# Hybrid encoder, one core: opening sums on column tiles, three projection groups by quarters, GpSimd's tensor work on VectorE

## The chip, the cores and the metric

One core of one Trainium2 chip runs the whole kernel. The metric is device time in microseconds; the kernel before takes 831.13 us, the median of three runs (829.75 to 832.08). Matrices are float32; a product is made either directly in fp32, which TensorE does in two passes, or from a split of both operands into a high part (fp32r) and a low part, which takes three passes: high by high, high by low, low by high.

## The reference, cut to what matters

Two layers work on x of 256 tokens by 1024 channels. The conditioning vector c (1024) gives scale, shift and gate for both sub-layers by one matrix product.

```
mod = silu(c) @ ada_w + ada_b                      # ada_w (1024, 6144)
sh_m, sc_m, g_m, sh_f, sc_f, g_f = split(mod, 6)
h = rms_norm(x, norm_mix_g) * (1 + sc_m) + sh_m
proj = h @ w_in                                    # qa ka va | cq ckv kr | qc | kc vc | ga gb gc
o_na  = neighborhood_attention(qa, ka, va, rpb)    # 4 heads of 64
o_mla = attention from rms_norm(cq) @ w_uq, rms_norm(ckv) @ w_ukv, rope(kr)   # 4 heads
o_gqa = attention from rms_norm + axial rope of qc, kc; vc                    # 8 heads, 2 kv heads
merged = sig(ga)*(o_na @ w_na) + sig(gb)*(o_mla @ w_mla) + sig(gc)*(o_gqa @ w_gqa)
x = x + g_m * (merged @ w_out)
h = rms_norm(x, norm_ffn_g) * (1 + sc_f) + sh_f
x = x + g_f * ((silu(gate) * up) @ w_down)         # gate, up = split(h @ w_gate_up)
```

After two layers a last rms_norm gives the output.

## The kernel before, in words

**Items.** A projection is a *group* (line 285): up to 512 output columns, contracted in units of 256 rows. Each unit is an *item*: one weight tile of 128 x 2 x 512, loaded on SP's queue, split by `load_split` (line 269; high part on ScalarE, line 215, low part on VectorE, line 216), and used in two *steps*, one per 128 tokens (t = 0, 1). A step of a split item is 6 matmuls (lines 305 to 307); of an item marked native, 2 fp32 matmuls in two passes each (line 298). After the last unit the group's `post` function reads the accumulated bank.

**Order of the work.** The loop at the end walks the items: it runs the side work hung on that item (`at`), loads and splits, runs the first step and keeps the second back until four items are pending (LAG); for the first eight items the second step follows at once. `later(k, f)` puts f k steps back; `flush` empties the pending steps. This order is a priority: the framework that builds the program schedules each engine's instructions from it, so that a ready instruction may pass one that waits. SP's queue issues all loads.

**The opening of layer 0.** `first_a` loads the first quarter of the scale columns (two tiles of 512 KB), x, and the first quarter of the shift columns; it takes the sum of squares of x on ScalarE (line 220), scales x on VectorE (230), transposes it on TensorE (237) and copies it to SBUF (877). `first_q(q)` treats a quarter, 256 of the 1024 columns of scale and shift: `ada_quarter_dve` (148) multiplies weight tiles by the conditioning column and accumulates on VectorE (lines 137, 139), 8 operations of 128 x 256 per quarter of scale or shift, then reduces over partitions by transposes (121) and a VectorE reduction (123). Quarter 0 of shift alone goes through TensorE as a row (161, 167). Then ScalarE makes the modulated operand hF (894), and it is split for later groups. Groups g1 (columns 768 to 1183) and ga (0 to 511) are native and interleaved by quarters: items 0 to 7. Group gc (keys and values, split) follows as items 8 to 11, then w_uq, w_ukv, and gd (queries of the grouped attention) as items 14 to 17; six gate groups follow and, spread among them, the attention pairs in the order na, mla, gqa.

**GpSimd** does the rotary tables of `params` (363, 369; at item 0), the bias of the neighbourhood attention (386; at item 8, after four loads of 256 KB), the rotary key of the latent attention (428 to 432), the merge adds (706), the last norm's product (827), and small powers for the norms (107). The merge (line 695 on) multiplies each branch by its gate on VectorE (701, 705), adds on GpSimd (706), and transposes the sum on TensorE (715) for w_out.

**PSUM** has eight banks: four for groups (`psmm`), three for transposes and the like (`tpb`), one for attention outputs (`pso`).

The lines that the steps rest on:

```python
def group(...):                               # line 305 on, for each of 2 row blocks of a unit
    nc.tensor.matmul(ps[t], lhs(t, 0, kc), hi[:, j, 0:n], ...)
    nc.tensor.matmul(ps[t], lhs(t, 0, kc), lo[:, j, 0:n], ...)
    nc.tensor.matmul(ps[t], lhs(t, 1, kc), hi[:, j, 0:n], ...)
# attention output: two heads on two column tiles, line 666
nc.tensor.matmul(ov[i * 64:(i + 1) * 64, j, :], v, ptTs[i][:, k, :], ...)
```

Of the kernel before, what the change touches and what calls it, by code (L numbers as in the profile page):

```python
# [31 lines left out]
SD = 2  # L32
# [5 lines left out]
def encoder_kernel(ctx: ExitStack, tc: tile.TileContext, x, consts, cols, rows, ada_b, rpb, ada_w, w_in,  # L38
# [102 lines left out]

    def ada_quarter_load(l, m, q, u):
        c0 = m * D + q * 256
        raw = t4([P, 4, 256])
        nc.sync.dma_start(raw, ada_w[l, u * 512:(u + 1) * 512, c0:c0 + 256].rearrange("(k p) n -> p k n", p=P))
        return raw

    def ada_quarter_dve(l, ms, q, raws):
        accs = {m: modp.tile([P, 512], F32, tag="acc", name=nm("acc"))[:, 0:256] for m in ms}
        for kc in range(KC):  # L150
            for m in ms:
                ada_acc(accs[m], raws[(m, kc // 4)][:, kc % 4:kc % 4 + 1, :], kc, 1)
        for m in ms:
            col_mod(l, m, q * 2, 2, accs[m])

    def ada_quarter_pe(l, m, q, raws):
        if (l, m) not in mods:
            mods[(l, m)] = modp.tile([P, KC], F32, tag=f"c{m}", name=nm("cm"))
        ps = tpb()
        for kc in range(KC):  # L160
            nc.tensor.matmul(ps[0:1, 0:256], sc[:, kc:kc + 1], raws[(m, kc // 4)][:, kc % 4, :], start=(kc == 0),
                             stop=(kc == KC - 1))
        row = t2([1, 256])
        nc.scalar.copy(row, ps[0:1, 0:256])
        pc = tpb()
        for j in range(2):
            nc.tensor.matmul(pc[:, j:j + 1], row[0:1, j * P:(j + 1) * P], ones[0:1, 0:1], start=True, stop=True)
        nc.vector.tensor_tensor(out=mods[(l, m)][:, q * 2:q * 2 + 2], in0=pc[:, 0:2],
                                in1=colp(l, "b", m * KC + q * 2, 2), op=ALU.add)
# [115 lines left out]
    def group(units_src, nkc, n, lhs, post, kc0=0, pres=None):  # L285
# [3 lines left out]
        for u in range(nu):  # L289
            nk = min(2, nkc - 2 * u)  # L290

            def mm(t, it, u=u, nk=nk):
                if u == 0:
                    ps[t] = psmm.tile([P, 512], F32, tag="mm", name=nm("mm"))
                if it.get("native"):
                    for j in range(nk):
                        kc = 2 * u + j
                        nc.tensor.matmul(ps[t][:, 0:n], state["hF"][kc // 4][:, kc % 4, t * P:(t + 1) * P],  # L298
                                         it["w"][:, j, 0:n], start=(kc == 0), stop=(kc == nkc - 1))
                    return  # L300
# [45 lines left out]
    def layer(l):  # L346
# [6 lines left out]
        def params():  # L353
# [5 lines left out]
            for nme, g0 in (("q", 0), ("k", 64)):  # L359
# [3 lines left out]
                nc.gpsimd.tensor_tensor(out=gC, in0=axC, in1=g.unsqueeze(1).to_broadcast([P, NT, 64]), op=ALU.mult)  # L363
# [11 lines left out]
        def na_bias():  # L375
            st["bias"] = []
            for t in range(NT):
# [622 lines left out]
```

## Time and profile before

| | us |
|---|---|
| median of three runs | 831.13 |
| lowest, highest | 829.75, 832.08 |
| the profiled execution's own time | 831.54 |
| its span, first to last instruction | 829.7 |
| mean granted TensorE clock | 0.991 |

The profile is of one execution. In the rows below, PE is TensorE's matmul side, PEld its weight loads, DVE is VectorE, ACT ScalarE, POOL GpSimd; L12 is line 12. Times are us from the start of the span. A matmul's end is modelled with its drain, so the spacing of starts, not the length of one, is its cost in a row of matmuls. An fp32 matmul is recorded as two passes.

### The profile page before, as it was taken

To read this page: it belongs to the slowest core of one execution; us is meant where nothing else is said; L and a number is where in the kernel's file an instruction comes from. 1 tells how busy PE (TensorE), PEld (TensorE's weight loads), DVE (VectorE), ACT (ScalarE), POOL (GpSimd) and SP (SyncE) were. 2 spreads that over 40 slices of the span, in tenths; PEclk is the share of its full clock that TensorE was granted. 3 is DMA by queue.
4 is the path that set the end of the run, shared out by engine and by line. 5 is a ranking of instruction groups with operands and counts; after the bars stand their busy time and mean duration, and the time that the engine had idled before them with its cause. 6 is when DMAs were issued, how large, how long until landed. Compare 5 with 4: busy or idle time off the path is not lost.

```text
span 829.7 us, 10670 instructions
## 1 busy us (share of the span) xinstructions
PE 788.0 (95%) x3682; PEld 624.6 (75%) x3682; DVE 608.3 (73%) x926; ACT 450.6 (54%) x789; POOL 89.9 (11%) x110
## 2 busy tenths in 40 slices
PE   3789999999999999999999999999999999999996
PEld 2337777778778888888878877777877888888884
DVE  4859998798776888775566599879977667665562
ACT  3346886744366544344457688674447644444341
POOL 1125010003300000000033001000330000000010
PEclk9999999999999999999999999999999999999998
DMA  9977687788466999886874668778755777876531
GB/s 312 336 182 260 184 272 234 240 285 258 153 179 204 340 296 306 282 270 182 215 208 146 180 182 275 231 242 277 265 171 167 226 245 219 255 221 190 181 104 51
DMA packets 113158, 187.19 MB, mean 226 GB/s; under 512 B 14416, under 2 KB 34000, under 8 KB 113104
## 3 DMA queue, kind: packets, MB, share of 16 engines
q1 hardware_dynamic: 113104, 186.51, 72.1%
q8 instruction: 29, 0.48, 0.2%
q14 instruction: 25, 0.20, 0.1%
HBM read 185.44 MB, written 1.05 MB: 225 GB/s over the span
## 4 chain that ended last, share of the span: by engine, by line
PE 58%; DVE 5%; ACT 2%; DMA 2%; issue 2%; POOL 1%; POOLq 0%; DVEq 0%; ACTq 0%
PE mm L307 18%; PE mm L305 18%; PE mm L306 18%; DMA raw<-in_ada_w_dram 2%; DVE wlo L216 2%; PE tp L777 1%; ACT tm L246 1%; DVE acc L139 1%; PE o L666 0%; PE tp L237 0%; DVE sm L611 0%; PE tp L121 0%; ACT hi L215 0%; ACT whi L215 0%; PE tp L645 0%
## 5 line engine op out<-in xcount | busy, mean ns | idle before, releaser
L216 DVE TENSOR_TENSOR wlo<-raw,whi 128x1024 fp32r<-128x1024 f32 (+2 forms) x240 | 299.6, 1254 | 103.7 <-ACT whi L215 103.4
L215 ACT CAST whi<-raw 128x1024 fp32r<-128x1024 f32 (+2 forms) x240 | 249.4, 1044 | 226.4 <-PE mm L307 140.4
L305 PE MATMUL mm<-whi,hi 128*128 128x512 f32 (+1 forms) x768 | 307.5, 401 | 0.6 <-ACT hi L215 0.6
L307 PE MATMUL mm<-whi,lo 128*128 128x512 f32 (+1 forms) x768 | 301.2, 392 | 0.4 <-DVE lo L719 0.2
L306 PE MATMUL mm<-wlo,hi 128*128 128x512 f32 (+1 forms) x768 | 299.5, 390 | 0.9 <-DVE wlo L216 0.9
L307 PEld LDWEIGHTS mm<-whi,lo 128*128 128x128 f32 x768 | 144.5, 188 | 32.9 <-DVE lo L216 1.7
L305 PEld LDWEIGHTS mm<-whi,hi 128*128 128x128 f32 x768 | 144.7, 189 | 31.3 <-issue 3.5
L306 PEld LDWEIGHTS mm<-wlo,hi 128*128 128x128 f32 x768 | 144.9, 189 | 28.5 <-DVE wlo L216 1.1
L139 DVE SCALAR_TENSOR_TENSOR acc<-raw,sc,acc 128x512 f32<-128x512 f32 x140 | 104.8, 749 | 26.9 <-DMA raw<-in_ada_w_dram 25.3
L305 PE MATMUL mm<-whi,s 128*128 128x512 f32 (+1 forms) x188 | 73.6, 391 | 0.0
L307 PE MATMUL mm<-whi,s 128*128 128x512 f32 (+1 forms) x188 | 72.8, 388 | 0.0
L306 PE MATMUL mm<-wlo,s 128*128 128x512 f32 (+1 forms) x188 | 72.8, 387 | 0.0
L706 POOL TENSOR_TENSOR tm<-tm,tm 128x512 f32<-128x512 f32 x16 | 30.4, 1901 | 194.9 <-DVE tm L705 188.5
L307 PEld LDWEIGHTS mm<-whi,s 128*128 128x128 f32 x188 | 35.3, 188 | 7.1
L306 PEld LDWEIGHTS mm<-wlo,s 128*128 128x128 f32 x188 | 35.3, 188 | 6.8
L305 PEld LDWEIGHTS mm<-whi,s 128*128 128x128 f32 x188 | 35.3, 188 | 6.9
L386 POOL TENSOR_TENSOR s<-s,con 128x256 f32<-128x256 f32 x16 | 15.6, 1008 | 174.1 <-DMA s<-in_rpb_dram 174.1
L629 ACT ACTIVATE P<-P,sm 128x256 f32<-128x256 f32 x64 | 29.2, 508 | 4.3 <-DVE sm L627 4.0
L107 POOL TENSOR_TENSOR sm<-sm,nhalf 128x1 f32<-128x1 f32 (+2 forms) x22 | 19.1, 867 | 107.8 <-DVE sm L499 42.1
L298 PE MATMUL mm<-raw,hF 128*128 128x416 f32 (+1 forms) x64 | 28.9, 605 | 0.0
L624 ACT ACTIVATE P<-tp,sm,rq 128x256 f32<-128x256 f32 x32 | 17.8, 560 | 18.0 <-DVE sm L621 13.4
L237 PE MATMUL tp<-con,tm 128*128 128x128 f32 x64 | 10.1, 313 | 17.7 <-DVE tm L230 17.7
(143 smaller groups left out, 680.4 us busy)
## 6 DMA issues: line engine op xcount, KB each, us to landing
raw<-in_ada_w_dram SPq DMA_DIRECT2D x80, 512.0 KB, 4.7
raw<-in_w_gu_dram SPq DMA_DIRECT2D x80, 512.0 KB, 4.4
raw<-in_w_in_dram SPq DMA_DIRECT2D x64, 512.0 KB, 4.5
raw<-in_w_dn_dram SPq DMA_DIRECT2D x44, 512.0 KB, 4.8
s<-in_ada_w_dram SPq DMA_DIRECT2D x16, 512.0 KB, 9.3
raw<-in_w_out_dram SPq DMA_DIRECT2D x16, 512.0 KB, 4.7
raw<-in_w_in_dram SPq DMA_DIRECT2D x16, 256.0 KB, 3.8
raw<-in_w_gqa_dram SPq DMA_DIRECT2D x8, 512.0 KB, 5.3
```

The lines of the kernel that those rows point to most:

```text
L107: nc.gpsimd.tensor_tensor(out=r, in0=ms, in1=nhalf[:, 0:n], op=ALU.pow)
L139: nc.vector.scalar_tensor_tensor(out=acc, in0=raw[:, j, :], scalar=sc[:, kc:kc + 1], in1=acc, op0=ALU.mult, op1=ALU.add)
L215: nc.scalar.copy(hi_ap, src)
L216: nc.vector.tensor_tensor(out=lo_ap, in0=src, in1=hi_ap.bitcast(F32), op=ALU.subtract)
L298: nc.tensor.matmul(ps[t][:, 0:n], state["hF"][kc // 4][:, kc % 4, t * P:(t + 1) * P], it["w"][:, j, 0:n], start=(kc == 0), stop=(kc == nkc ...
L305: nc.tensor.matmul(ps[t][:, 0:n], lhs(t, 0, kc), hi[:, j, 0:n], start=first, stop=False)
L306: nc.tensor.matmul(ps[t][:, 0:n], lhs(t, 0, kc), lo[:, j, 0:n], start=False, stop=False)
L307: nc.tensor.matmul(ps[t][:, 0:n], lhs(t, 1, kc), hi[:, j, 0:n], start=False, stop=last)
L386: nc.gpsimd.tensor_tensor(out=b[:, 4 * h:4 * h + 4, :], in0=rev[:, 4 * h:4 * h + 4, :], in1=mask.unsqueeze(1).to_broadcast([P, 4, W]), op= ...
L624: nc.scalar.activation(pt[:, t, :], src[:, t, :], AF.Exp, bias=nb[:, t:t + 1], scale=scale[t], accum_out=rs[:, t:t + 1])
L629: nc.scalar.activation(pt[:, t, :], pt[:, t, :], AF.Copy, scale=rc[:, t:t + 1])
L706: nc.gpsimd.tensor_tensor(out=m, in0=m, in1=y, op=ALU.add)
```

## The change

- Loads: x comes right after the conditioning columns, ahead of the constants.
- Scale and shift sums of layer 0: a quarter's weights come in four tiles, each with 256 rows of scale and shift side by side (eight loads of 256 KB). The conditioning vector is laid out with 32 columns per row block, of which the first holds it and the others are zero. Eight fp32 matmuls of 32 stationary and 512 moving columns accumulate on four column tiles of the array (tile j takes row blocks j and j + 4). ScalarE copies the bank, four matmuls with a column of ones sum the tiles and turn the row into columns, and VectorE adds bias and norm gain. The high part of the operand comes straight from ScalarE, the low part from VectorE (multiply-add, then subtract).
- Groups g1, ga and gc are all split and interleaved by quarters: items 0 to 11, both steps of an item at once. Group gc takes the attention bank and one transpose bank. Quarter q + 1 is loaded and summed at the second item of quarter q and reduced at the third; TensorE's instructions of these 12 items keep the written order (`manual_schedule`).
- Layer 0: gd comes before w_uq and w_ukv; attention in the order na, gqa, mla; `params` at item 7, `na_bias` at item 12; gd's transposes 3 steps after instead of 8.
- All GpSimd tensor work but the powers, the norm's sums and one small scaling goes to VectorE, in both layers.

The diff, cut to its core (the native path and the old quarter functions are removed whole):

```diff
@@
+    for t in range(NT):
+        nc.sync.dma_start(x_sb[:, t, :], x[t * P:(t + 1) * P, :])
     NCON = consts.shape[1]
...
-    def group(units_src, nkc, n, lhs, post, kc0=0, pres=None):
+    def group(units_src, nkc, n, lhs, post, bank=None):
...
-                    ps[t] = psmm.tile([P, 512], F32, tag="mm", name=nm("mm"))
+                    ps[t] = bank(t) if bank else psmm.tile([P, 512], F32, tag="mm", name=nm("mm"))
...
-                nc.gpsimd.tensor_tensor(out=gC, in0=axC, in1=g.unsqueeze(1).to_broadcast([P, NT, 64]), op=ALU.mult)
+                nc.vector.tensor_tensor(out=gC, in0=axC, in1=g.unsqueeze(1).to_broadcast([P, NT, 64]), op=ALU.mult)
...
-                    nc.gpsimd.tensor_tensor(out=b[:, 4 * h:4 * h + 4, :], in0=rev[:, 4 * h:4 * h + 4, :],
+                    nc.vector.tensor_tensor(out=b[:, 4 * h:4 * h + 4, :], in0=rev[:, 4 * h:4 * h + 4, :],
...
-            later(DEF, b_)
+            later(3 if l == 0 else DEF, b_)
...
         group(lambda u: [win[u * 256:(u + 1) * 256, 512:768], win[u * 256:(u + 1) * 256, 1696:1952]], 8, 512, hlhs,
-              post_gc)
+              post_gc, bank=(lambda t: tpb() if t else pso.tile([P, 512], F32, tag="o", name=nm("o"))) if l == 0 else None)
         if l == 0:
-            a, b = items[i0:i0 + 4], items[i0 + 4:i0 + 8]
-            items[i0:i0 + 8] = [v for ab in zip(a, b) for v in ab]
-            for v in items[i0:i0 + 8]:
-                v["native"] = True
+            g = [items[i0 + 4 * j:i0 + 4 * j + 4] for j in range(3)]
+            items[i0:i0 + 12] = [v for abc in zip(*g) for v in abc]
+            group(kslice(win, 1184, 512), 8, 512, hlhs, post_gd)
...
-        for br in ("na", "mla", "gqa"):
+        for br in ("na", "gqa", "mla") if l == 0 else ("na", "mla", "gqa"):
...
-        at(i0, params)
-        at(i0 + 8, na_bias)
+        at(i0 + (7 if l == 0 else 0), params)
+        at(i0 + (12 if l == 0 else 8), na_bias)
...
-                nc.gpsimd.tensor_tensor(out=m, in0=m, in1=y, op=ALU.add)
+                nc.vector.tensor_tensor(out=m, in0=m, in1=y, op=ALU.add)
...
+    def first_loads(q):
+        raws = []
+        for v in range(4):
+            raw = t4([P, 2, 2, 256])
+            for mi, m in enumerate((1, 0)):
+                c0 = m * D + q * 256
+                nc.sync.dma_start(raw[:, :, mi, :], ada_w[0, v * 256:(v + 1) * 256, c0:c0 + 256].rearrange(
+                    "(k p) n -> p k n", p=P))
+            raws.append(raw.rearrange("p k m n -> p k (m n)"))
+        return raws
+
+    scz = ppl.tile([P, KC, 32], F32, tag="pp", name="scz")
+    nc.vector.memset(scz, 0.0)
+    nc.vector.tensor_copy(scz[:, :, 0], sc)
+
+    def first_sums(q, raws):
+        ps = tpb()
+        for kc in range(KC):
+            j = kc % 4
+            nc.tensor.matmul(ps[32 * j:32 * j + 32, :], scz[:, kc, :], raws[kc // 2][:, kc % 2, :], start=(kc < 4),
+                             stop=(kc >= 4), tile_position=(0, 32 * j))
+        four = t2([P, 512])
+        nc.scalar.copy(four, ps)
+        return four
+
+    def first_mod(q, four):
+        red = tpb()
+        for j in range(4):
+            nc.tensor.matmul(red[:, j:j + 1], four[:, j * P:(j + 1) * P], ones, start=True, stop=True)
...
+        full = t2([P, 2, S])
         for j in range(2):
+            kc = k0 + j
+            xv = xT0[q // 2][:, kc % 4, :]
+            nc.scalar.activation(hT[0][:, kc, :], xv, AF.Identity, scale=A[:, kc:kc + 1], bias=B[:, kc:kc + 1])
+            nc.vector.tensor_scalar(out=full[:, j, :], in0=xv, scalar1=A[:, kc:kc + 1], scalar2=B[:, kc:kc + 1],
+                                    op0=ALU.mult, op1=ALU.add)
+        for j in range(2):
+            kc = k0 + j
+            nc.vector.tensor_tensor(out=hT[1][:, kc, :], in0=full[:, j, :], in1=hT[0][:, kc, :].bitcast(F32),
+                                    op=ALU.subtract)
...
         load_split(it)
+        if i < 12:
+            q1 = i // 3 + 1
+            if i % 3 == 1 and q1 < 4:
+                raws = first_loads(q1)
+            with tc.manual_schedule(engines={mybir.EngineType.PE}):
+                if i % 3 == 1 and q1 < 4:
+                    four = first_sums(q1, raws)
+                if i % 3 == 2 and q1 < 4:
+                    first_mod(q1, four)
+                step(0, i)
+                step(1, i)
+            continue
         if len(pend) >= LAG:
```

## Rows read from the trace of the kernel before

**Rows 1.** The page's first part: busy us (share), instructions of each engine.

```profile
PE 788.0 (95%) x3682; PEld 624.6 (75%) x3682; DVE 608.3 (73%) x926; ACT 450.6 (54%) x789; POOL 89.9 (11%) x110
```

**Rows 2.** Busy us (instructions) by engine in stretches; granted clock, DMA share, GB/s.

```profile
0.00:10.00 10.00, 0.00 (x0) 0.00 (x0) 2.73 (x9) 1.49 (x2) 0.19 (x4) 1.00 0.79 259
10.00:20.00 10.00, 6.48 (x26) 4.47 (x27) 5.27 (x14) 5.01 (x12) 2.02 (x4) 1.00 1.10 358
20.00:30.00 10.00, 7.08 (x25) 3.65 (x23) 8.02 (x22) 3.10 (x8) 3.28 (x10) 0.83 1.08 366
30.00:40.00 10.00, 7.98 (x24) 3.80 (x23) 9.11 (x24) 2.96 (x8) 0.00 (x0) 1.00 1.03 347
0.00:70.00 70.00, 46.65 (x151) 26.05 (x152) 44.63 (x98) 25.17 (x54) 18.22 (x32) 0.95 0.88 262
```

**Rows 3.** Timeline of the opening: start, us, instruction [idle before, releaser].

```profile
10.56 0.63 ACT L220 ACTIVATE tm<-x_sb 128x512 f32<-128x512 f32 x1 [7.66 <-DMA x_sb<-in_x_dram]
...
13.52 3.68 PE L237 MATMUL tp<-con,tm 128*128 128x128 f32 x16 [13.52 <-DVE tm L230]
...
22.51 0.60 PE L167 MATMUL tp<-ones,tm 1*128 1x1 f32 x4 [0.51 <-ACT tm L164]
...
49.35 10.84 PE L298 MATMUL mm<-raw,hF 128*128 128x416 f32 x26
...
62.84 0.60 PE L444 MATMUL tp<-con,tm 128*128 128x128 f32 x4
64.35 0.50 PE L306 MATMUL mm<-wlo,hi 128*128 128x512 f32 x1 [0.91 <-DVE wlo L216]
```

**Rows 4.** Who waited for whom: us in total, times, longest.

```profile
ACT hF L894 <- DVE cm L131: 20.0, 3, 9.1
```

**Rows 5.** Groups of the first 100 us, by shape: busy us, mean ns.

```profile
L139 DVE SCALAR_TENSOR_TENSOR acc<-s,sc,acc 128x256 f32<-128x256 f32 x49 | 22.7, 493 | 2.0 <-DMA s<-in_ada_w_dram 1.2
...
L137 DVE TENSOR_SCALAR acc<-s,sc 128x256 f32<-128x256 f32 x7 | 2.4, 347 | 5.1 <-DMA s<-in_ada_w_dram 5.1
L877 ACT COPY xT<-tp 128x512 f32<-128x512 f32 x4 | 2.3, 586 | 2.2 <-PE tp L237 2.2
```

**Rows 6.** Busy us of each engine in two later stretches.

```profile
64.00:200.00 136.00, 134.65 (x685) 105.29 (x686) 120.79 (x211) 92.58 (x187) 19.45 (x18) 1.00 0.80 252
90.00:110.00 20.00, 19.72 (x105) 15.24 (x104) 19.93 (x41) 18.67 (x46) 3.68 (x4) 1.00 0.64 189
```

**Rows 7.** Timeline of TensorE around an attention output on two column tiles.

```profile
106.01 0.39 PE L306 MATMUL mm<-wlo,hi 128*128 128x512 f32 x1
106.24 0.39 PE L307 MATMUL mm<-whi,lo 128*128 128x512 f32 x1
106.56 1.08 PE L666 MATMUL o<-PT,s 128*64 128x256 f32 x8
```

**Rows 8.** VectorE's groups over the whole run, by shape.

```profile
L216 DVE TENSOR_TENSOR wlo<-raw,whi 128x1024 fp32r<-128x1024 f32 x232 | 292.1, 1264 | 96.5 <-ACT whi L215 96.1
...
L460 DVE TENSOR_TENSOR tm<-tm,tm 128x512 f32<-128x512 f32 x4 | 2.7, 678 | 0.0
...
L605 DVE SCALAR_TENSOR_TENSOR P<-tp,s 128x256 f32<-128x256 f32 x16 | 5.9, 412 | 0.0
...
L458 DVE TENSOR_TENSOR tm<-s,gS 128x64 f32<-128x64 f32 x8 | 1.6, 218 | 0.0
```

**Rows 9.** GpSimd's groups over the whole run, by shape.

```profile
L706 POOL TENSOR_TENSOR tm<-tm,tm 128x512 f32<-128x512 f32 x16 | 30.4, 1901 | 194.9 <-DVE tm L705 188.5 <-DVE cm L131 6.0
```

**Rows 10.** Timeline at the end of layer 1's merge, VectorE and GpSimd.

```profile
604.21 2.12 DVE L216 TENSOR_TENSOR wlo<-raw,whi 128x1024 fp32r<-128x1024 f32 x1 [0.17 <-ACT whi L215]
...
606.85 1.21 DVE L216 TENSOR_TENSOR wlo<-raw,whi 128x1024 fp32r<-128x1024 f32 x1
...
611.65 2.11 POOL L706 TENSOR_TENSOR tm<-tm,tm 128x512 f32<-128x512 f32 x1 [2.42 <-DVE tm L705]
```

**Rows 11.** DMA issues by line: KB each, median us to landing.

```profile
s<-in_rpb_dram SPq DMA_DIRECT2D x8, 256.0 KB, 5.3
```

More of the change, by code (lines that the diff above doesn't have):

```diff
@@ L31 @@
 DM = 4
-SD = 2
 DG = 4
@@ L140, in ada_acc @@
                                                op0=ALU.mult, op1=ALU.add)
[L142 to L169, printed above, removed]
     def ada_units(l, m, hf, row):
@@ L276, in load_split @@
             c += w
-        if it.get("native"):
-            it["w"] = raw
-            return
         hi = spl.tile([P, 2, 512], F32R, tag="whi", name=nm("whi"))
@@ L293, in mm @@
                 if u == 0:
-                    ps[t] = psmm.tile([P, 512], F32, tag="mm", name=nm("mm"))
[L295 to L300, printed above, removed]
+                    ps[t] = bank(t) if bank else psmm.tile([P, 512], F32, tag="mm", name=nm("mm"))
                 hi, lo = it["w"]
@@ L860, in encoder_kernel, with first_x @@
     xT0 = {}
-    rawq = {}
-    def first_a():
-        for u in range(2):
-            rawq[(1, u)] = ada_quarter_load(0, 1, 0, u)
-        for t in range(NT):
-            nc.sync.dma_start(x_sb[:, t, :], x[t * P:(t + 1) * P, :])
-        for u in range(2):
-            rawq[(0, u)] = ada_quarter_load(0, 0, 0, u)
+    def first_x():
+        xT = act.tile([P, KC, S], F32, tag="lo", name=nm("xT"))
+        for hf in range(2):
+            xT0[hf] = xT[:, hf * 4:hf * 4 + 4, :]
         for t in range(NT):
@@ L875, in first_a @@
             for hf in range(2):
-                xT0[(t, hf)] = ppl.tile([P, 4, P], F32, tag="pp", name=nm("xT"))
-                nc.scalar.copy(xT0[(t, hf)], transposed(x_scaled(t, r, hf)))
+                nc.scalar.copy(xT0[hf][:, :, t * P:(t + 1) * P], transposed(x_scaled(t, r, hf)))
         state[0]["hT"] = act_tiles()
-    def first_q(q):
-        if q == 0:
-            ada_quarter_dve(0, (1,), 0, rawq)
-            ada_quarter_pe(0, 0, 0, rawq)
-        else:
-            raws = {(m, u): ada_quarter_load(0, m, q, u) for u in range(2) for m in (1, 0)}
-            ada_quarter_dve(0, (1, 0), q, raws)
-        A, B, hT = mods[(0, 1)], mods[(0, 0)], state[0]["hT"]
-        if q % 2 == 0:
-            state.setdefault("hF", []).append(spl.tile([P, 4, S], F32, tag="wlo" if q else "whi", name=nm("hF")))
-        hF = state["hF"][q // 2]
-        for j in range(2):
-            kc = 2 * q + j
-            for t in range(NT):
-                nc.scalar.activation(hF[:, kc % 4, t * P:(t + 1) * P], xT0[(t, q // 2)][:, kc % 4, :], AF.Identity,
-                                     scale=A[:, kc:kc + 1], bias=B[:, kc:kc + 1])
-        k0 = (2 * q) % 4
-        later(SD, lambda: split_to(hT[0][:, 2 * q:2 * q + 2, :], hT[1][:, 2 * q:2 * q + 2, :], hF[:, k0:k0 + 2, :]))
@@ new lines, in first_mod @@
+    def first_mod(q, four):
+        red = tpb()
+        for j in range(4):
+            nc.tensor.matmul(red[:, j:j + 1], four[:, j * P:(j + 1) * P], ones, start=True, stop=True)
+        k0 = 2 * q
+        A, B, hT = mods[(0, 1)], mods[(0, 0)], state[0]["hT"]
+        r2 = sm(2)
+        nc.vector.tensor_tensor(out=r2, in0=red[:, 0:2], in1=colp(0, "b", KC + k0, 2), op=ALU.add)
+        nc.vector.scalar_tensor_tensor(out=A[:, k0:k0 + 2], in0=r2, scalar=1.0, in1=colp(0, "gm", k0, 2), op0=ALU.add,
+                                       op1=ALU.mult)
+        nc.vector.tensor_tensor(out=B[:, k0:k0 + 2], in0=red[:, 2:4], in1=colp(0, "b", k0, 2), op=ALU.add)
+        full = t2([P, 2, S])
+        for j in range(2):
+            kc = k0 + j
[7 more added lines that the diff above has]
+                                    op=ALU.subtract)
@@ L915, in encoder_kernel @@
         if i == 0:
-            first_a()
-            first_q(0)
-        if i < 6 and i % 2 == 0:
-            first_q(i // 2 + 1)
+            raws = first_loads(0)
+            first_x()
+            first_mod(0, first_sums(0, raws))
         for f in side.get(i, ()):
@@ L926, in encoder_kernel @@
         pend.append(i)
-        if i < 8:
-            step(1, pend.pop(0))
     while pend:
```

17 lines of the change are left out of this document (9 added, 8 removed).

## The prediction, made before the change was run

> **What bounds the kernel now.** I read the page first: TensorE is busy for 788.0 of 829.7 us [rows 1], so the time is TensorE's work plus its holes. The table by stretches then shows where the holes are. TensorE is busy for 46.65 of the first 70 us, so 23.4 of the 41.7 idle us lie there, while from 10 to 40 us DMA moves 347 to 366 GB/s and VectorE's share climbs to 9.1 of 10 us [rows 2]. Third, the timeline of that stretch: x reaches ScalarE at 10.56, and from 64.35 on the split matmuls run without a large hole [rows 3]. Fourth, what ScalarE waits for in the opening: 20.0 us in three waits of up to 9.1 for the shift column that VectorE finishes [rows 4]; and VectorE spends 49 x 493 ns = 22.7 us on accumulating 128x256 pieces (and 7 x 347 ns on the first of each) [rows 5]. So the opening is set by the scale and shift sums on VectorE, not by TensorE or by DMA. After it TensorE sets the time, with VectorE 120.79 of 136 us busy from 64 to 200 [rows 6].
>
> **The change, part by part.** All sums run to a point in the program: the three groups g1, ga and gc done. What follows them is the same work.
>
> *The sums.* The 56 VectorE accumulations, the 7 transposed reductions and the one row-wise quarter go. Each quarter becomes 8 fp32 matmuls of 32 stationary and 512 moving columns, two passes each, on four column tiles. In the native phase 26 passes of 416 and 512 columns take 10.84 us, 0.42 us each [rows 3], so 16 passes one behind the other are 6.7 us. Do the tiles run side by side? The attention output is such a case with two column tiles: 8 passes of 256 columns, each half of 0.42, would take 1.7 us in turn and have ended after 1.08 [rows 7], of which a modelled drain is part. So two tiles halve the time, and I take 6.7 / 4 = 1.7 us a quarter; 6.7 is the other end. Changing to column tiles costs little there: the last full matmul starts at 106.24, the first tiled one 0.32 later, where full ones follow each other by 0.23 [rows 7].
>
> The Trainium skill speaks against this step twice. "TensorE: Matmul & The Clock Gate" (Part 3: Packing small matmuls) says that a weight load overlaps a running matmul only where its row group differs, and all four tiles here use all rows; yet it gives 2.38x for three column tiles, by which four would need some 2.1 us a quarter (an estimate), 1.6 us more in all. "TensorEngine Tiling (Array Packing)" (Key Properties) says that a mode switch drains TensorE. By the row, 1.08 us for 8 passes, the tiles do overlap and a switch costs about 0.1 us.
>
> *The chain of a quarter.* Sums, then a 128x512 copy on ScalarE (0.59 us [rows 5]), 8 one-column passes (four took 0.60 [rows 3]; 0.6 to 1.2), three small VectorE operations, together some 0.6 (0.22 is the row of a 128x64 one [rows 8]), then the high part on ScalarE (about 0.5, between its 128x128 and 128x512) beside 128x256 multiply-add and subtract on VectorE (0.35 and 0.41 each [rows 5, 8]). That is about 5.5 us with the sums. Only the first quarter's chain is bare; later ones lie beside an item of 12 passes (2.7 us at 0.23), as the fixed order puts sums ahead of the second item, reduction ahead of the third.
>
> *The groups.* g1 and ga lose 64 native passes (0.42 each, 27 us) for 96 split ones of 0.23 or, for 416 columns, 0.19: 20 us. Eight more weight splits come to VectorE (1.26 each [rows 8]) and ScalarE, in a stretch where 25 us of accumulation left.
>
> *DMA.* By the code the new order needs 3.51 MB up to quarter 0 (cols 0.07, x 1.05, constants 0.29, quarter 2.10), then 3.05, 3.57 and 3.57 MB for the next quarters with the items between, and 2.0 MB for the last four items. Against what the old run had moved by 10, 20, 30 and 40 us (2.59, 6.17, 9.83, 13.30 MB [rows 2]), and with 0.5 us for landing, the quarters arrive at 13, 21.5, 31.5 and 41.5 us, the last weights at 47. Twice as many issues on SP (256 KB each) are still faster than the bytes.
>
> *TensorE's time line.* x is now ahead of constants and quarters, so it lands near 7; from landing to the last transpose took 10.56 to 17.2 [rows 3], so this ends near 13.6, with quarter 0. Its chain ends at 19; item 0 at 21.5 to 22.5. From there sums (1.7), three items (7.7) and the reduction (0.6) follow three times, with hardly a wait: 10.0 each, to 52; the last two items (2.7 each) end at 57.5. Shorter waits may take some off, a slow start may add (the granted clock was 0.83, a mean of 1.2 and 2.4 GHz, from 20 to 30 us [rows 2]), and so may late splits: I take **58 us** (54 to 66). Group gc holds one of the three transpose banks until its end; sums and reductions have the other two, and nothing else asks for one before.
>
> *After it.* Before, from 64.35 to the end were 765.35 us; in them lay 46 gc passes (10.4 us), and 14 transposes had been done that now follow (four took 0.60 with the drain [rows 3], so some 1.5 us). Remaining: 756.4.
>
> *GpSimd to VectorE.* The 16 merge adds of 128x512 cost GpSimd 1.9 us and will cost VectorE 0.68 each, as will the two at the end; the 16 of 128x256, 0.41; the 36 small ones some 0.2 [rows 8, 9]: 26 us more on VectorE over the run. But GpSimd also stretches VectorE: with an add running a weight split took 2.12 us, another soon after 1.21 [rows 10]; if each of the 16 adds does that to one split, 15 of the 26 us come back. At the end of each merge TensorE waits for the add: 2.11 us in the row, now 0.68 [rows 8, 10]. Two layers: -2.9 us. Bounds 0 and -6.
>
> *VectorE's load behind the opening.* From 64 to 200 it was idle for 15 us. That stretch will be some 9 us shorter, with 5 us of bias, rotary and merge work added, and 3 of gc splits gone. Idle falls to about 4. Taken: +3 us of TensorE waits (0 to 10). On SP's queue three steps move. The two parameter loads go from item 0 to item 7, behind two quarters, yet some 20 us ahead of item 9, which wants them, and the bias loads landed in 5.3 [rows 11]: nothing. The four bias loads (1 MB) go from item 8 to item 12, behind the last quarter and right ahead of the query group's weights; at 5.3 us to land these come up to 5 us later than they could, near 54, and their splits are ready at 56 to 58, just as TensorE wants them: in the 0 to 10. That group's four loads pass those of the two low-rank weights, which are wanted later now. Layer 0's attention order moves no work: nothing for it.
>
> *Sum:* 58 + 756.4 - 2.9 + 3 = 814.5 us of span. The profiled execution took 831.54 for 829.7, so 1.8 more: **816**. The median of the runs is 831.13, 0.05% below the profiled one, which I ignore.
>
> **Rivals.**
> 1. *Tiles in turn.* Each pass waits for its own weights and a quarter's sums cost 6.7 us: 4 x 5.0 more on a TensorE that is by then the bound, so the groups end at 78 and the time is 832 with less VectorE pressure behind it (-2.9, +0). Against it: the attention row. For it: no row has four tiles with full rows. 10%. By the Trainium skill's rule on weight loads, cited above, it would come out this way.
> 2. *VectorE becomes the bound* in layer 0's attention: if it needs its old 11% of idle, about 122 us of work take 136 where TensorE offers 127. +9 in place of +3: 822. For it, 19.93 of 20 us busy at 90 to 110 [rows 6]; against it, TensorE ran on through these. 14%.
> 3. *The fixed order stops TensorE* (the slower side). With nothing allowed to pass a waiting sum or reduction, the copy may stand behind weight casts that wait for DMA, and the operand behind four splits (5 us) on VectorE. If nothing overlaps, a quarter is 7.7 of matmuls and 1.7 + 0.6 + 0.6 + 0.6 + 2 + 5 of chain, 18 us; four from 13.6 end at 86: 86 + 753.5 + 1.8 = 841. It decides from 4.5 us per quarter on, which would eat the 18 us between 58 and 76. Against it: 2.7 us of matmuls stand between sums and reduction. 7%.
>
> **How the numbers follow.** The forecast has 69%, the rivals 10, 14 and 7. 0.3% is about what a measurement of this kernel can tell from no change: 828.6 to 833.6. The forecast and rival 2 are faster; rival 1 is the same, and half of the opening's slow tail; rival 3 is slower: 0.82, 0.10, 0.08. The range: 54 for the opening, -6 for the merges and 0 for VectorE give 54 + 756.4 - 6 + 1.8 = 806. At the high end 66 for the opening and +6 behind it: 66 + 756.4 - 2.9 + 6 + 1.8 = 827, rounded up to 828; rivals 1 and 3 stay out.
>
> **What would show it.** Right: four sums passes starting within nanoseconds, a quarter's 16 in under 2.5 us; the last gc matmul at 55 to 61; DMA above 340 GB/s up to 45 us; no split over 1.3 us at the merges, and the transposes there waiting under 1 us. Wrong: sums of 6 us, casts ahead of the copy with TensorE waiting for it, or VectorE full and holes of some us between 60 and 180.

## The result, and the profile after

The changed kernel takes 822.05 us, the median of four runs (821.38 to 823.06), against 831.61 for the kernel before beside it (829.75 to 833.66). The ratio is 0.9886, 95% interval 0.9859 to 0.9912: 1.1% faster, 6 us above the forecast of 816. One run of `e10_no_bias` (2035.91 us) and one of the kernel before (1329.57 us) took far longer than all others of their kernel and are left out of every median below, so `e10_no_bias` stands at 815.55 and not at the 816.6 that an expectation names. The profiled execution took 822.51 us for a span of 820.4 (before 831.54 for 829.7).

The page's first part, which answers to [rows 1], and the column heads are busy us (share), instructions of each engine:

```profile
PE 790.7 (96%) x3776; PEld 633.4 (77%) x3776; DVE 598.8 (73%) x955; ACT 453.7 (55%) x788; POOL 25.8 (3%) x40
```

GpSimd falls from 89.9 to 25.8 us, and VectorE falls too, from 608.3 to 598.8, though it took the work: the accumulations of the opening are gone. TensorE's holes shrink from 41.7 to 29.7 us.

The stretches that answer to [rows 2, 6], busy us of PE, PEld, DVE, ACT, POOL, then granted clock, DMA share and GB/s:

```profile
10.00:20.00 10.00, 7.76 (x36) 4.45 (x36) 3.50 (x9) 4.98 (x8) 0.00 (x0) 0.84 1.09 361
20.00:30.00 10.00, 10.00 (x50) 6.92 (x50) 2.74 (x6) 3.12 (x5) 0.00 (x0) 0.82 1.10 361
30.00:40.00 10.00, 10.00 (x59) 7.40 (x58) 4.27 (x11) 3.59 (x6) 0.00 (x0) 1.00 1.08 357
...
70.00:80.00 10.00, 6.93 (x30) 5.02 (x29) 9.97 (x24) 6.88 (x12) 2.87 (x2) 0.91 0.95 284
80.00:90.00 10.00, 9.88 (x53) 7.43 (x52) 9.45 (x29) 7.74 (x21) 2.24 (x2) 0.92 0.45 127
...
64.00:200.00 136.00, 131.28 (x657) 100.06 (x656) 119.46 (x228) 88.71 (x182) 6.61 (x6) 0.99 0.79 243
...
0.00:70.00 70.00, 59.94 (x303) 45.27 (x304) 35.62 (x91) 35.42 (x62) 5.15 (x12) 0.95 0.97 302
```

TensorE's idle time of the first 70 us is 10.1 instead of 23.4 us, and from 20 to 40 us it has no hole at all. But a new one has opened right behind: 6.93 of 10 busy from 70 to 80, at a clock of 0.91, with VectorE at 9.97. From 64 to 200 TensorE is busy 131.28 us where it was 134.65.

TensorE's timeline of the opening, which answers to [rows 3, 7] (start, us, instruction, idle time before it and its releaser):

```profile
7.82 3.68 PE L209 MATMUL tp<-con,tm 128*128 128x128 f32 x16 [7.82 <-DVE tm L202]
11.42 3.14 PE L861 MATMUL tp<-s,scz 128*32 128x512 f32 x16
15.30 1.05 PE L870 MATMUL tp<-ones,tm 128*128 128x1 f32 x8 [0.73 <-ACT tm L864]
17.49 0.72 PE L268 MATMUL mm<-whi,hi 128*128 128x416 f32 x1 [1.14 <-ACT hi L882]
...
22.69 2.36 PE L861 MATMUL tp<-s,scz 128*32 128x512 f32 x16
...
33.84 1.92 PE L861 MATMUL tp<-s,scz 128*32 128x512 f32 x16
35.69 0.50 PE L268 MATMUL mm<-whi,hi 128*128 128x512 f32 x1
...
60.38 0.39 PE L270 MATMUL tp<-whi,lo 128*128 128x512 f32 x1
60.61 0.39 PE L268 MATMUL mm<-whi,hi 128*128 128x512 f32 x1
```

A quarter's 16 passes (line 861) take 1.92 us in the last two quarters, at a granted clock of 1.00; the second takes 2.36 and the first 3.14. In the third quarter the passes start in fours, four within 0.02 us (33.84 to 33.86), the next four 0.45 us later, and the weights of the next four are loaded (33.86 to 33.88) while the first four run. The last gc matmul (into `tp`) starts at 60.38; at 60.61 gd goes on.

The hole, in the same view:

```profile
72.41 0.39 PE L270 MATMUL mm<-whi,lo 128*128 128x512 f32 x1
73.23 0.44 PE L268 MATMUL mm<-whi,s 128*128 128x384 f32 x1 [0.44 <-ACT s L187]
73.52 0.34 PE L269 MATMUL mm<-wlo,s 128*128 128x384 f32 x1
74.11 0.66 PE L407 MATMUL tp<-con,tm 128*128 128x128 f32 x4 [0.25 <-ACT s L408]
77.14 0.44 PE L270 MATMUL mm<-whi,s 128*128 128x384 f32 x1 [2.38 <-DVE s L188]
...
78.54 0.63 PE L269 MATMUL mm<-wlo,s 128*128 128x512 f32 x1
78.96 0.63 PE L270 MATMUL mm<-whi,s 128*128 128x512 f32 x1
```

Group w_uq has its weights (`whi`, `wlo`) but not its stationary operand `s`, the normed and transposed latent. From 78.1 on the 512-column matmuls follow each other by 0.42 us instead of 0.23. The granted clock is 0.91 and 0.92 in the two 10 us rows above, which is 3.4 us at the lower of TensorE's two levels (1.2 and 2.4 GHz; in the trace 78.24 to 81.65). Before it fell, TensorE had stood for 3.0 of the 4.3 us from 72.8 to 77.1. What VectorE did ahead of the low part of `s`:

```profile
72.25 0.76 DVE L421 TENSOR_TENSOR tm<-tm,gS 128x256 f32<-128x256 f32 x2
72.93 2.35 DVE L188 TENSOR_TENSOR wlo<-raw,whi 128x1024 fp32r<-128x1024 f32 x2
75.20 1.42 DVE L349 TENSOR_TENSOR s<-s,con 128x256 f32<-128x256 f32 x4
76.54 1.01 DVE L188 TENSOR_TENSOR s<-tp,s 128x384 fp32r<-128x384 f32 x2
```

And ScalarE ahead of the high part; the latent's transposes (line 383) had started on TensorE at 64.70:

```profile
66.99 0.31 ACT L430 ACTIVATE tm<-s 128x128 f32<-128x128 f32 x1 [1.41 <-PE tp L383]
69.41 0.59 ACT L456 COPY tm<-mm 128x512 f32<-128x512 f32 x1 [2.11 <-DVE tm L393]
70.29 0.63 ACT L458 ACTIVATE tm<-tm 128x512 f32<-128x512 f32 x1 [0.29 <-DVE kpe L395]
70.83 1.99 ACT L187 CAST whi<-raw 128x1024 fp32r<-128x1024 f32 x2
72.72 0.85 ACT L187 CAST s<-tp 128x384 fp32r<-128x384 f32 x2
```

So 12.4 us pass from the operand's first transpose (64.70) to the first matmul that takes its low part (77.14), mostly in the queues of two engines. In the kernel before the cast came at 71.7 after transposes from 60.0, as slow, but gc lay between: its matmuls filled TensorE up to 72.6, where w_uq began without a wait.

The merges, on VectorE at the end of layer 1's, which answers to [rows 10]:

```profile
601.89 1.23 DVE L188 TENSOR_TENSOR wlo<-raw,whi 128x1024 fp32r<-128x1024 f32 x1
603.02 0.70 DVE L669 TENSOR_TENSOR tm<-tm,tm 128x512 f32<-128x512 f32 x1
603.63 2.37 DVE L188 TENSOR_TENSOR wlo<-raw,whi 128x1024 fp32r<-128x1024 f32 x2
```

The addition takes 0.70 us, a split 1.23, and two of them 2.37; in [rows 10] one took 2.12 and the addition 2.11 on GpSimd.

The times to common points of the program show where the gain stands (starts on TensorE, us, before and after; the gap is the kernel's lead):

| | before | after | lead |
|---|---|---|---|
| g1, ga, gc done (before: 829.7 less the 756.4 that follow) | 73.3 | 60.4 | 12.9 |
| first attention output, layer 0 | 106.6 | 99.1 | 7.5 |
| last attention output, layer 0 | 174.6 | 170.2 | 4.4 |
| first transpose of layer 0's merge | 200.2 | 195.8 | 4.4 |
| first transpose of x after it | 240.3 | 231.7 | 8.6 |
| first transpose of layer 1's merge | 594.3 | 586.8 | 7.5 |
| first transpose of x after it | 632.0 | 622.7 | 9.3 |
| end | 829.7 | 820.4 | 9.3 |

The opening brought 12.9 us, 8.5 of them went again by the end of layer 0's attention (5.4 of these by its first output), and the two merges brought 4.2 and 1.8. That the first merge brought more than the second has a cause in the kernel before: there the wait for the addition in layer 0 was followed by a lower clock, in layer 1 not.

```profile
220.33 0.86 PE L715 MATMUL tp<-con,tm 128*128 128x128 f32 x4 [1.65 <-POOL tm L706]
...
220.00:230.00 10.00, 9.67 (x38) 7.96 (x39) 4.06 (x5) 3.32 (x5) 0.27 (x1) 0.83 0.32 92
```

The granted clock of 0.83 over 10 us is 3.4 us at the lower level, half of them lost: some 1.7 us of the 4.2. In the changed kernel the granted clock stays at 1.00 there.

### The profile page after: what moved, and what is told of

Read it like the earlier page. It is cut to its first block, busy times and chain, and to the rows that moved or that the text cites. A ratio compares the mean times of both kernels' runs of the same rounds, so it can differ in the third digit from the quotient of the medians.

```text
span 820.4 us, 10803 instructions
## 1 busy us (share of the span) xinstructions
PE 790.7 (96%) x3776; PEld 633.4 (77%) x3776; DVE 598.8 (73%) x955; ACT 453.7 (55%) x788; POOL 25.8 (3%) x40
## 4 chain that ended last, share of the span: by engine, by line
issue 49%; PE 31%; DVE 8%; DMA 6%; ACT 4%; POOL 1%; POOLq 0%; DVEq 0%; ACTq 0%
PE mm L268 8%; PE mm L270 8%; PE mm L269 8%; DMA raw<-in_ada_w_dram 6%; DVE wlo L188 2%; DVE acc L140 2%; PE tp L861 1%; POOL sm L108 1%; PE o L629 1%; ACT P L587 1%; ACT tm L218 1%; DVE sm L574 1%; PE tp L209 1%; PE tp L608 1%; PE tp L560 1%
## 5 line engine op out<-in xcount | busy, mean ns | idle before, releaser
L187 ACT CAST whi<-raw 128x1024 fp32r<-128x1024 f32 (+2 forms) x248 | 256.9, 1041 | 221.6 <-PE mm L270 137.1
L268 PE MATMUL mm<-whi,hi 128*128 128x512 f32 (+1 forms) x784 | 314.0, 400 | 1.8 <-ACT hi L882 1.1
L270 PE MATMUL mm<-whi,lo 128*128 128x512 f32 (+1 forms) x784 | 307.1, 392 | 0.2
L269 PE MATMUL mm<-wlo,hi 128*128 128x512 f32 (+1 forms) x784 | 306.1, 390 | 0.5 <-DVE wlo L188 0.4
L268 PEld LDWEIGHTS mm<-whi,hi 128*128 128x128 f32 x784 | 148.1, 189 | 34.7 <-issue 5.7
L269 PEld LDWEIGHTS mm<-wlo,hi 128*128 128x128 f32 x784 | 148.3, 189 | 28.9 <-DVE wlo L188 1.7
L270 PE MATMUL mm<-whi,s 128*128 128x512 f32 (+1 forms) x188 | 73.3, 390 | 2.4 <-DVE s L188 2.4
L197 POOL TENSOR_SCALAR sm<-ss 128x1 f32<-128x1 f32 x10 | 4.0, 404 | 662.4 <-ACT tm L192 662.4
L218 ACT ACTIVATE tm<-tp,cm,cm 128x128 f32<-128x128 f32 x48 | 21.3, 472 | 6.2 <-PE tp L209 6.2
L192 ACT ACTIVATE tm<-x_sb 128x512 f32<-128x512 f32 x20 | 12.6, 632 | 16.8 <-DVE x_sb L703 14.6
L733 DVE TENSOR_TENSOR tm<-tm,mm 128x512 f32<-128x512 f32 (+1 forms) x24 | 15.4, 640 | 8.7 <-PE mm L270 7.1
```

Of the source, the lines that this page charges most:

```text
L187: nc.scalar.copy(hi_ap, src)
L192: nc.scalar.activation(junk, x_sb[:, t, hf * 512:(hf + 1) * 512], AF.Square, scale=1.0 / 32.0, accum_out=ss[:, hf:hf + 1])
L218: nc.scalar.activation(fv[:, j, :], xT[:, j, :], AF.Identity, scale=A[:, kc:kc + 1], bias=B[:, kc:kc + 1])
L268: nc.tensor.matmul(ps[t][:, 0:n], lhs(t, 0, kc), hi[:, j, 0:n], start=first, stop=False)
L269: nc.tensor.matmul(ps[t][:, 0:n], lhs(t, 0, kc), lo[:, j, 0:n], start=False, stop=False)
L270: nc.tensor.matmul(ps[t][:, 0:n], lhs(t, 1, kc), hi[:, j, 0:n], start=False, stop=last)
```

## The experiments

The question was the 8.5 us. The theories, as the expectations use them: A, the bias additions (line 349) in VectorE's queue are the whole cause; B, the new order of layer 0 as such, which C makes precise; C, latency: the operand of w_uq comes late, and with gc moved into the opening too little work (gd alone) lies between; D, VectorE is full in that stretch, whatever waits. All edits are against the changed kernel unless said otherwise. The kernel before took 830.4 us beside the first four runs (`e1_bias` to `e4_one_tile`), 830.06 beside the next four (`e5_moves`, `e8_late_lr`, `e9_kpe_now`, `e10_no_bias`), 829.75 beside the last.

**One move back at a time.** The three moves to VectorE that lie in or after the hole, each given back to GpSimd.

```diff
-nc.vector.tensor_tensor(out=b[:, 4 * h:4 * h + 4, :], in0=rev[:, 4 * h:4 * h + 4, :],   # e1_bias, line 349
+nc.gpsimd.tensor_tensor(out=b[:, 4 * h:4 * h + 4, :], in0=rev[:, 4 * h:4 * h + 4, :],
-nc.vector.tensor_tensor(out=a, in0=kr, in1=mlC[:, t, :], op=ALU.mult)     # e2_kpe, all four of lines 391 to 395
+nc.gpsimd.tensor_tensor(out=a, in0=kr, in1=mlC[:, t, :], op=ALU.mult)
-nc.vector.tensor_tensor(out=m, in0=m, in1=y, op=ALU.add)                  # e3_merge, line 669
+nc.gpsimd.tensor_tensor(out=m, in0=m, in1=y, op=ALU.add)
```

> The changed kernel with the eight bias additions per layer back on GpSimd. Theory A (the 8 us given back between 60 and 170 us come from VectorE's queue, where the bias additions stand ahead of the low part of the latent operand for which TensorE waits 2.4 us): the hole at 72 to 77 us falls from 3.6 to under 2 us and the time from 822.0 to 818 to 820. Theory B (they come from the new order of layer 0, with the query group and the grouped attention earlier): the hole stays or moves, 821 to 823.

Measured 822.91 us (0.9909, 0.9876 to 0.9942): nothing gained. VectorE was rid of 2.8 us of bias additions, yet the low part of the operand starts at 75.90 instead of 76.54. VectorE's timeline of this run, and then what TensorE waited for from 60 to 85 us (us in total, times, longest):

```profile
69.19 1.56 DVE L440 TENSOR_TENSOR tm<-tm,sm 128x128 f32<-128x128 f32 x2 [0.22 <-POOL sm L108]
70.67 0.72 DVE L395 TENSOR_TENSOR kpe<-tm 128x32 f32<-128x32 f32 x1
...
75.90 1.01 DVE L188 TENSOR_TENSOR s<-tp,s 128x384 fp32r<-128x384 f32 x2
...
PE mm L268 <- ACT s L187: 2.0, 1, 2.0
PE tp L407 <- DVE s L188: 1.3, 1, 1.3
```

Line 440 takes 1.56 us for what took 0.49, line 395 0.72 for 0.19, while GpSimd adds (69.13 to 72.0). Even so VectorE is busy for 17.11 us from 58 to 78 where it was 18.67, and the hole stays: now TensorE waits for ScalarE's high part first. So A isn't borne out as the whole cause. The run isn't a pure removal, since the additions on GpSimd slow VectorE, and with it the rotary key that ScalarE's queue waits for.

> The changed kernel with the four rotary key operations per token block back on GpSimd. Theory A says that they hold a buffer for which ScalarE waits 2.1 us at 69.4 us, ahead of the latent operand's cast: the hole shrinks, 819 to 821. Theory B: 821 to 823. A third way: GpSimd's own slow small operations (0.5 to 1.2 us each) come later than VectorE's and the key is late, 823 or more.

Measured 820.8 us (0.9896, 0.9852 to 0.994), 1.2 under the changed kernel with intervals that overlap: at most a small part. The hole stays (3.2 us for the low part).

> The changed kernel with the 16 merge additions back on GpSimd. By the marks along the two traces the merges gave 2.3 + 1.9 us in layer 0 and 1.8 in layer 1, so the time rises by 4 to 6, to 826 to 828. If the gain at the merges came from something else (a later, shorter queue behind the attention), it stays within 1 us of 822.

Measured 829.14 us (0.9986, 0.9968 to 1.0005): 7 us lost, more than the 4 to 6 expected and most of the change's gain. By the common points layer 0's merge brings 1.5 us of lead and layer 1's loses 0.4, instead of 4.2 and 1.8. Another 1.5 us are lost by the last attention output of layer 0, before the first of these additions (190.8); their cause is open. TensorE waits for the addition again:

```profile
608.17 2.11 POOL L669 TENSOR_TENSOR tm<-tm,tm 128x512 f32<-128x512 f32 x1 [2.42 <-DVE tm L668]
...
610.34 0.65 PE L678 MATMUL tp<-con,tm 128*128 128x128 f32 x4 [1.59 <-POOL tm L669]
```

**The sums on one column tile**, all eight row blocks in turn (the disputed price of rival 1).

```diff
-nc.tensor.matmul(ps[32 * j:32 * j + 32, :], scz[:, kc, :], ..., start=(kc < 4), stop=(kc >= 4), tile_position=(0, 32 * j))
+nc.tensor.matmul(ps[0:32, :], scz[:, kc, :], ..., start=(kc == 0), stop=(kc == KC - 1), tile_position=(0, 0))
```

> The changed kernel with all eight sum products of a quarter on one column tile, one behind the other, so that a quarter's 16 passes take 6.8 us in place of 1.8. If side by side is what the tiles give and TensorE is the bound of the opening: +18 to +20 us, 840 to 842. If DMA is the bound of the opening and hides part of it: +6 to +12, 828 to 834.

Measured 838.93 us (1.0102, 1.0047 to 1.0157), slower than the kernel before, and 1 us under the range for TensorE as the bound. A quarter's sums now take, in TensorE's timeline,

```profile
39.97 7.05 PE L861 MATMUL tp<-s,scz 128*32 128x512 f32 x16
...
56.08 7.05 PE L861 MATMUL tp<-s,scz 128*32 128x512 f32 x16
```

7.05 us against 1.92, and gc is done at 77.3 instead of 60.4. The four tiles do run side by side, and the opening's gain hangs on it.

**The moves alone:** the kernel before, with its GpSimd arithmetic on VectorE and nothing else.

```diff
-nc.gpsimd.tensor_tensor(...)   # lines 363, 369, 386, 428 to 432, 706, 827 of the kernel before
+nc.vector.tensor_tensor(...)
```

> The kernel before with only GpSimd's tensor work put on VectorE, the opening and the order as they were. From the run that puts the merge additions back (829.1 against 822.0) the moves alone are worth some 5 to 7 us: 824 to 827. If they help only behind the new opening, under 2 us: 829 to 831.

Measured 826.26 us (0.9947, 0.9927 to 0.9968): the moves give 3.8 us without the new opening. By the common points 3.1 of them are there at the first attention output, 2.3 at layer 0's merge, 6.5 after it and 6.3 after layer 1's; the profiled span ends 5.5 earlier. The two merges bring 4.2 and 1.8 here too. And this run has the same moves on VectorE, busy for 9.90 of 10 us from 70 to 80, beside a TensorE that is busy for all 10, with gc where it was: a full VectorE alone makes no hole there.

**Cover for the late operand:** layer 0's two low-rank groups come behind the first gate group, four items later; the attention's side work keeps its place.

```diff
+        def low_rank():
+            group(lambda u: [w_uq[l]], 2, 384, clhs(0), post_uq)
+            group(lambda u: [w_ukv[l]], 1, 512, clhs(2), post_ukv)
         if l == 0:
             ...
             group(kslice(win, 1184, 512), 8, 512, hlhs, post_gd)
-        group(lambda u: [w_uq[l]], 2, 384, clhs(0), post_uq)
-        group(lambda u: [w_ukv[l]], 1, 512, clhs(2), post_ukv)
         if l > 0:
+            low_rank()
             group(kslice(win, 1184, 512), 8, 512, hlhs, post_gd)
-        iG = len(items)
+        iG = len(items) + (2 if l == 0 else 0)
         ...
         for gi in range(6):
             group(kslice(win, 1952 + gi * 512, 512), 8, 512, hlhs, post_gate(gi))
+            if l == 0 and gi == 0:
+                low_rank()
```

> The changed kernel with layer 0's two low-rank groups four items later, behind the first gate group. Theory C (the hole at 72 to 77 us is one of latency: the latent operand goes transposes at 64.7, cast on ScalarE at 72.7, low part on VectorE at 77, and only the query group of 11 us stands between): the hole goes, 2 to 4 us of TensorE's wait and a clock drop with it, 817 to 820. Theory D (ScalarE and VectorE are full from 55 to 90 us, so that TensorE waits for one thing or another): the hole comes elsewhere, 821 to 823.

Measured 815.74 us (0.9821, 0.9806 to 0.9837): 6.3 us faster than the changed kernel, more than C expected. Of the runs that leave no work out only `e13_late_kpe`, built on it, is as fast. The operand comes no sooner (cast at 72.2, low part at 75.6), but w_uq now starts at 79.7, and the stretches show no hole and the full clock:

```profile
70.00:80.00 10.00, 10.00 (x50) 8.31 (x48) 7.05 (x16) 4.58 (x9) 2.00 (x2) 1.00 0.61 192
80.00:90.00 10.00, 9.92 (x51) 7.73 (x51) 10.00 (x26) 9.17 (x21) 2.34 (x2) 1.00 0.51 177
64.00:200.00 136.00, 134.45 (x689) 105.04 (x688) 125.29 (x238) 91.78 (x186) 5.83 (x6) 1.00 0.79 249
```

VectorE is busy 125.29 of 136 us from 64 to 200, more than in the changed kernel, and TensorE 134.45: VectorE had room. The additions of line 349 still stand right ahead of the low part (74.26, for 1.42 us) and cost nothing once there is cover. C predicts this, D doesn't.

**A shorter latency.** First the rotary key at once in the function behind g1, so that ScalarE's copy at line 456 needn't wait for it:

```diff
+            nc.vector.tensor_tensor(out=a, in0=kr, in1=mlC[:, t, :], op=ALU.mult)   # e9_kpe_now: with its three
+            ...                                                                     # followers, ahead of b_
```

> The changed kernel with the rotary key made at once in the first group's end, not nine steps later, so that its two buffers of the shared pool come free early. If ScalarE's waits of 2.1 us for that pool at 69 us are what delays the latent operand's cast (theory C, in that form): the cast comes 2 us earlier and the time falls by 1 to 3 us, 819 to 821. Theory D: 821 to 823.

Measured 821.7 us (0.9884, 0.986 to 0.9907): no change. The cast comes 1.8 us sooner (70.9), the low part later (77.5), and TensorE waits 4.8 us for it: sooner in one queue isn't enough. Then without the bias additions:

```diff
-                b = t4([P, 16, W])
-                ...
-                st["bias"].append(b)
+                st["bias"].append(hk)      # e10_no_bias
```

> The changed kernel without the neighbourhood bias additions at all: the loaded bias is used as it lies, without reversal and without the mask, in both layers; the loads stay. It takes 2.8 us of VectorE's work out of each layer and brings none to GpSimd. Theory D (VectorE's work as such is the bound behind the opening): 2 to 4 us less, 818 to 820. Theory C: the low part comes 1.4 us earlier at most, 820.5 to 822.

Measured 815.55 us (0.9829, 0.9809 to 0.985), under the ranges of both theories. Here the low part comes at 68.2, 8 us sooner, far more than the 2.8 us of additions that had stood ahead of it: ScalarE's built order has changed, and the cast at 66.60 stands ahead of the copy of line 456 (451 in this kernel). This speaks for a latency made of two queues, but D would also gain from work left out. The two edits together tell them apart:

> The changed kernel with layer 0's low-rank groups four items later and without the bias additions: the reversal and the mask of the relative bias are left out in both layers, the bias is used as it is loaded, and the loads stay. Each of the two edits alone gave about 6 us (815.7 and 816.6 against 822.1). If both closed the same hole behind the opening (theory C: the latent operand comes late, and nothing covers TensorE), the second adds little: 813 to 816. If VectorE's queue behind the opening is a loss of its own (theory D: VectorE is full there), the two add up: 809 to 811.

Measured 816.56 us (0.9856, 0.9832 to 0.988), no better than either alone; D wanted 809 to 811. Both close the same hole, and the granted clock stays at 1.00 from 60 to 90 us: C.

**Two attempts at more**, both on top of the low-rank groups' new place: the bias additions at item 9, and the rotary key back on GpSimd (the edit of `e2_kpe`).

```diff
-        at(i0 + (12 if l == 0 else 8), na_bias)
+        at(i0 + (9 if l == 0 else 8), na_bias)     # e12_late_early
```

> The changed kernel with layer 0's low-rank groups four items later and the bias additions issued three items sooner. Theory C: the hole is closed already, so 814 to 817, no change against 815.7. Theory D: the bias additions sooner come off the stretch in which VectorE is full, 811 to 813.

Measured 823.45 us (0.993, 0.9915 to 0.9945). Neither theory had this. With the bias in the opening, DMA moves 263 GB/s from 40 to 50 us where it moved 307, TensorE waits for splits at the last items, and gc is done at 66.4 instead of the 59.9 of `e8_late_lr`:

```profile
54.05 0.46 PE L269 MATMUL mm<-wlo,hi 128*128 128x416 f32 x1 [1.24 <-DVE wlo L188]
...
59.99 0.52 PE L383 MATMUL tp<-con,tm 128*128 128x128 f32 x3 [0.52 <-DVE tm L374]
60.82 0.49 PE L268 MATMUL o<-whi,hi 128*128 128x512 f32 x1 [0.31 <-ACT whi L187]
62.64 0.50 PE L269 MATMUL o<-wlo,hi 128*128 128x512 f32 x1 [1.32 <-DVE wlo L188]
```

The splits that end the two longest waits stand on VectorE right behind bias additions (51.64 and 60.02, 1.4 us each), so late loads and additions in the way aren't separated. The granted clock is 0.83 from 60 to 70 us, so that a lower clock followed here as well.

> The changed kernel with layer 0's low-rank groups four items later and the rotary key's arithmetic back on GpSimd. Theory C: the hole is closed, 815 to 817. Theory D: VectorE loses some 3 us of work in the stretch behind the opening, 811 to 814.

Measured 815.7 us (0.9841, 0.9819 to 0.9863), no change against 815.74: taking these operations off VectorE gains nothing.

**TensorE's order left to the scheduler** (rival 3).

```diff
-            with tc.manual_schedule(engines={mybir.EngineType.PE}):
+            if True:
```

> The changed kernel with TensorE's written-out order taken away, so that the scheduler places the matmuls as it does in the kernel before. If the fixed order stops TensorE (rival 3 of the prediction), 3 us or more come back: 819 or less. If the fixed order costs nothing and gives nothing, 821 to 823. If it is worth something of its own (the order puts the sums and the first groups where the operands arrive), 824 or more, and the gc group ends later than 60.4.

Measured 834.21 us (1.0062, 1.0044 to 1.008): 12 us slower, slower than the kernel before, and all of it is in the opening, as gc is done at 72.1, 11.7 later, and the span ends 11.8 later. In TensorE's timeline quarter 1's sums fall into pieces between the matmuls of an item:

```profile
21.88 1.83 PE L861 MATMUL tp<-s,scz 128*32 128x512 f32 x8
...
25.44 1.05 PE L861 MATMUL tp<-s,scz 128*32 128x512 f32 x4
...
27.32 1.05 PE L861 MATMUL tp<-s,scz 128*32 128x512 f32 x4
...
29.06 1.05 PE L870 MATMUL tp<-ones,tm 128*128 128x1 f32 x8
32.13 0.50 PE L268 MATMUL o<-whi,hi 128*128 128x512 f32 x1 [2.02 <-ACT whi L187]
```

A quarter's next sums start 17.9 us later (21.88 to 39.73) where the written order takes 11.2 (22.69 to 33.84). In this run ScalarE's cast of the next item comes at 31.05, behind the copy of the sums at 28.42, for which ScalarE had waited 9.14 us; in the changed kernel the copy comes at 25.12 and the cast at 25.60. That the split-up sums hold back ScalarE's queue fits the rows; no run separates it from other effects of the free order.

## Why the prediction was right or wrong

It said 816 (806 to 828), faster; measured 822. Against its sum of 814.5 us of span there are 820.4, and that they are so near is in part luck: three terms cost 9.0 us more than forecast, and the merges gave 3.1 more. By its terms, from the table of common points:

| term, us | forecast | measured |
|---|---|---|
| opening, to the end of gc | 58 | 60.4 |
| behind the opening, to the end of layer 0's attention | +3 | +8.5 |
| merges | -2.9 | -6.0 (4.2 and 1.8) |
| between the two merges | 0 | +1.1 |

- **Sums on column tiles: right.** 1.92 us with the drain against 1.7, and 7.05 in turn against 6.7. Rival 1's price, 20 us for four quarters, came out as 16.9 at the end of gc and 15.5 at the end of the span. (Its 832 is a span; with the 1.8 us that the prediction adds elsewhere it is 833.) The rule of the Trainium skill ("TensorE: Matmul & The Clock Gate", Part 3) that a weight load overlaps a running matmul only in another row group does not hold for these four tiles of full rows: weights are loaded while passes on the same rows run, and four tiles are 3.7 times as fast as one. The estimate of 2.1 us from that page's 2.38x lies 0.2 above the row.
- **The opening: right within 2.4 us.** Item 0 ended at 22.7 where 22 was forecast, by two errors that cancel: x reached ScalarE at 4.86 instead of near 7 and the first sums started at 11.42 instead of 13.6, but item 0 took 5.2 us (17.49 to 22.69) instead of some 3, at a granted clock of 0.50 from 17.5 to 22.6. The quarters took 11.1 and 10.7 us instead of 10.0: the sums 1.85 us (2.29 in the second), the reduction 0.8, and the first matmul after sums or reduction 0.1 us longer. DMA kept 357 to 361 GB/s from 10 to 40 us.
- **The merges: right in mechanism, half too small.** No split at layer 1's merge is over 1.23 us where one took 2.12 [rows 10], and no transpose there waits. The forecast took 1.43 us for each end of a merge and let the stretched splits go free; the runs show 4.2 and 1.8. It had no term for the lower clock behind layer 0's merge, some 1.7 of the 4.2. By `e3_merge` this move carries some 5 of the change's 9 us, and 1.5 more that are lost ahead of the merges there.
- **Behind the opening: the step that failed.** The +3 was worked out from VectorE's idle time, and rival 2, which gives the measured 822, rests on the same quantity, so that its 822 is luck. The sign of being wrong that the prediction names came too: VectorE full (9.97 of 10 us) and a hole beside it. But the load was not the cause: taking work from VectorE and giving it to GpSimd changed nothing (`e1_bias`, `e13_late_kpe`), TensorE ran full beside a VectorE as busy in `e5_moves`, and so it did beside a busier VectorE once the low-rank groups stood later (`e8_late_lr`). The prediction had cost that group order in half a sentence ("wanted later now"). What it missed: w_uq hangs on g1 through a norm, transposes and splits, some 12 us through two queues in order, and the gc items that used to cover them had moved ahead. The hole costs twice: about 3.1 us of idle time from 70 to 80, and then 3.4 us at the lower clock level, half of them lost. That makes 4.8 of the 6.3 us that `e8_late_lr` gets back. The other 1.5 of these, the remaining 2 of the 8.5, and the 1.1 between the merges are not traced to a cause.
- **Rival 3 was wrong in its sign.** The written order costs nothing visible; it is worth 12 us, more than the whole gain. The prediction counted it as a risk and gave the free order no price.

## What to carry to other kernels

When a group is moved ahead to fill a hole, look at what it used to cover: follow the operand of the next dependent group through every queue and ask what work now lies between. A full engine beside a hole is not yet its cause; moving the waiting work later, with the engine's load unchanged, tells the two apart. Work that is left out, or given to another engine, changes the queues as well and tells less. Where small reductions gate the next stage, a written order of the tensor engine kept them whole here.

## What the runs showed of the hardware that was not expected

- GpSimd's additions stretch even small VectorE operations: 0.53 us more for a 128x32 one and for each of two 128x128 ones in `e1_bias`, and 0.89 more for a 128x1024 split at the merge of the kernel before (2.12 against 1.23). So giving work back to GpSimd gained VectorE nothing. The Trainium skill ("SBUF — State Buffer", "Who interferes with whom") says that a VectorE operation with two SBUF inputs and a reading GpSimd operation exclude each other; the rows agree in kind: the longer operations have two inputs in SBUF and lie beside GpSimd's additions.
- Short holes were followed by a lower clock, though not every time. 3.0 idle us in 4.3, the longest hole 2.4 us, were followed by 3.4 us at the lower level, with 512-column matmuls 0.42 us apart instead of 0.23; without the hole (`e8_late_lr`) the granted clock stayed at 1.00. In the kernel before one hole of 1.65 us at layer 0's merge was followed by 3.4 us at that level, while one of 1.6 us in the same place of `e3_merge` was not.
- With 1 MB of bias loads three items sooner (`e12_late_early`) the DMA moved 263 GB/s from 40 to 50 us where it moved 307, at a DMA share of 1.16 instead of 0.91.
